# Token tile 0's scaling on ScalarE with its residual added by a transfer, and the last tile's VectorE steps in another order

## The chip, the cores and the metric

The kernel runs on one core of one Trainium2 chip. Its time is device microseconds of one execution, and the median of several runs is quoted. Below, PE is TensorE, ACT is ScalarE, DVE is VectorE, POOL is GpSimd and SP is SyncE, which here only starts transfers.

## What is computed

One layer of an encoder trunk on 512 tokens of width 1024, in float32: a mixer and a feed-forward block, each with a root-mean-square norm before and behind it and a residual around it. What matters here is the last statement:

```python
h2 = _rmsnorm(x, g_pre_ffn)
x = x + _rmsnorm(_conv_gated_mlp(h2, w_up, conv_w, conv_b, w_down), g_post_ffn)
```

with `_rmsnorm(z, g) = z * rsqrt(mean(z * z) + EPS) * g`. So each row of the down projection's product z is squared and summed over its 1024 columns, one power gives its scale, and the row times the weights g times the scale is added to the residual row of x (called x1 in the kernel) and stored.

## The kernel before

The 512 tokens are four tiles of 128 rows, called tokens 0 to 3 in the code and here, and the 1024 columns are two halves of 512. All products are float32 made of three products of split operands, and TensorE runs through nearly the whole program. The down projection comes last, first for columns 0 to 511, then for columns 512 to 1023, each half by a Strassen-like scheme of seven products whose sums lie in eight PSUM banks. The second half ends with `token(t)`, called in the order 0, 2, 1, 3: token 0 inside `after6`, between two of the scheme's last products, the others behind the last product. Each call first starts the loads of the residual rows x1 from DRAM (line 1440, on SP's queue), then issues 24 matmuls (`add_whole`, line 1370) that complete two banks, 12 matmuls for each, and then the norm:

- `sums(i)` for i = 0, 1: DVE adds a PSUM bank and a partial sum to z (line 1452, 256 columns), ACT squares it and sums along the row (line 1454).
- `weighted(i)`: DVE multiplies z by the norm's weights into zs (line 1459).
- `first_sum()` (line 1462) and `scale()` (lines 1469 and 1470): DVE adds the four partial sums of squares in two steps (tiles q and qs, one column wide), and POOL raises the result to the power -0.5 (tile qr).
- `rows(...)`: DVE multiplies by the scale and adds the residual (line 1502), for columns 0 to 511 (tile zg) and 512 to 1023 (tile zs); each result is then stored (line 1505), from SP's queue or ACT's.

`rows` of one token is called within the next token's call; `ahead` carries what it needs. Columns 0 to 511 (zg) were weighted earlier, while the second half's products ran. A framework puts semaphores between engines and may reorder, but `keep_in_program_order` (`pin`) holds DVE's steps of tokens 1 and 3 as they are written. Each engine works through its own instructions in program order, and a transfer's start is one of them on SP, ACT or POOL. The names on DVE: q_8045, q_8047, q_8046 and q_8048 belong to tokens 0, 2, 1, 3, and so do zg_8240, zg_8368, zg_8304 and zg_8432.

Of the kernel before, what the change touches and what calls it, by code (L numbers as in the profile page):

```python
# [12 lines left out]
AF = mybir.ActivationFunctionType  # L13
ALU = mybir.AluOpType
# [3 lines left out]
S = 512  # L18
# [31 lines left out]
def tile_block(ctx: ExitStack, tc, xT, x, wall, par, cs, wsp, bsp, gpost, gffn, out):  # L50
    nc = tc.nc
# [10 lines left out]
    def blk(dt=F32, n="blk", shape=(P, S)):  # L62
        return sb.tile(list(shape), dt, tag="blk", bufs=NBLK, name=nm(n))
# [17 lines left out]
    def tmp(n="tmp", shape=(P, S)):  # L81
        return sb.tile(list(shape), F32, tag="tmp", bufs=6, name=nm(n))

    def halves(n):
        return [blk(n=n), blk(n=n)]

    def small(n, w, bufs=2):
        return sb.tile([P, w], F32, tag=n, bufs=bufs, name=nm(n))
# [4 lines left out]
    def const(n, shape):  # L93
        return sb.tile(list(shape), F32, tag=n, bufs=1, name=n)
# [182 lines left out]
    def w_get(look=LOOK):  # L277

        i = w_pos[0]
        w_pos[0] += 1  # L280
        room = 2 * look + (2 if w_size(units[i]) == 2 else 0)
        n = sum(w_size(u) for u in units[i : w_pos[1]])
        while w_pos[1] < len(units) and (w_pos[1] <= i or n + w_size(units[w_pos[1]]) <= max(room, 9 if look == LOOK else 0)):
            u = units[w_pos[1]]
            w_ready[w_pos[1]] = w_unit(u)
            w_pos[1] += 1
            n += w_size(u)
        return w_ready.pop(i)
# [106 lines left out]
    for k in range(KD):  # L395
# [4 lines left out]
        xt = xts[k]  # L400
# [55 lines left out]
    for t in range(NT):  # L456
        for n in range(2):
            xt = blk(n="x0")
            nc.sync.dma_start(xt, x[t, :, n * S : (n + 1) * S])
            nc.scalar.activation(  # L460
                out=xt, in_=xt, func=AF.Square, accum_out=ss[:, 4 * n + t : 4 * n + t + 1]
# [18 lines left out]
    for c in range(19, 1, -2):  # L480
        v.scalar_tensor_tensor(
            out=lc, in0=lc, scalar=1.0 / c, in1=lb, op0=ALU.add, op1=ALU.mult
        )
    v.scalar_tensor_tensor(out=lc, in0=lc, scalar=1.0, in1=la, op0=ALU.add, op1=ALU.mult)
    with behind():
        v.tensor_scalar(out=lg, in0=lgt, scalar1=0.0, scalar2=None, op0=ALU.min)
    v.scalar_tensor_tensor(
        out=lg, in0=lc, scalar=-2.0, in1=lg, op0=ALU.mult, op1=ALU.add
# [12 lines left out]
    for i, op in enumerate((ALU.max, ALU.min)):  # L501
        v.tensor_scalar(
            out=near[:, i * P : (i + 1) * P], in0=dist[:, P : 2 * P], scalar1=0.0, scalar2=None, op0=op
# [5 lines left out]
    zt = const("zt", [P, H, NT])  # L509
# [605 lines left out]
    x1 = [[dp_.tile([P, S], F32, tag=f"x1_{t}{n}", name=f"x1_{t}{n}") for n in range(2)] for t in range(NT)]  # L1115
# [36 lines left out]
    def turn(t, zs):  # L1152
        c = slice(t * 64, (t + 1) * 64)
        pf = []
        for n in range(2):
            p = ps()
            for f in range(4):
                pf.append(p[:, f * P : (f + 1) * P])
                nc.tensor.transpose(pf[-1], zs[n][:, f * P : (f + 1) * P], ident)
        for k in range(KD):  # L1160
            high = nc.scalar.activation(
                out=two(h2h[k])[:, :, c], in_=in_turn(pf[k]), func=AF.Copy, scale=col(FFNG + k)
            )
        for k in range(KD):
            last = v.scalar_tensor_tensor(
                out=two(h2l[k])[:, :, c], in0=in_turn(pf[k]), scalar=col(FFNG + k), in1=as32(two(h2h[k])[:, :, c]),
                op0=ALU.mult, op1=ALU.subtract,
            )
        return pf, high.ins, last.ins
# [26 lines left out]
    for t in range(NT):  # L1196
        acc = [dn_.finish(t, 0)]
        if t > 1:
            rows, _, last = turn(t - 2, zs[t - 2])
            if t == 2:  # L1200
                h2_rows(0, rows)
            with tc.issue_after(last):
                zs[t - 1] = scaled(*zs[t - 1])
        acc.append(dn_.finish(t, 1))
        zs[t], squared, ended = norms(t, acc)
        if t == 0:
            zs[0] = scaled(*zs[0])
    with tc.issue_after(squared):
        h2_rows(1, rows)
# [150 lines left out]
    def add_whole(m, t, gs, ws, last=False):  # L1360

        c = slice(t * P, (t + 1) * P)
        for n, b in enumerate(((M2, M3), (M4, M8))[t // 2]):
            o = m[b][:, (t % 2) * 256 : (t % 2 + 1) * 256]
            for g, (wh, wl) in zip(gs, ws):
                for k in range(2):
                    f = slice(k * S + n * 256, k * S + (n + 1) * 256)
                    ah, al = whole[2 * g + k]
                    for i, (a_, w_) in enumerate(((ah, wh), (ah, wl), (al, wh))):
                        nc.tensor.matmul(  # L1370
                            o, a_[:, c], turns(w_[:, f]), start=b == M8 and t == 2 and g == k == i == 0,
                            stop=last and g == gs[-1] and k == 1 and i == 2, skip_group_check=True,
                        )
# [60 lines left out]
    def token(t):  # L1434

        if not ww:
            ww.extend([w_get(), w_get()])
        xt = halves("x1")
        for n in range(2):
            nc.sync.dma_start(xt[n], x1[t][n])  # L1440
        add_whole(m, t, (0, 1), ww, True)
        z, zs_ = blk(n="z"), blk(n="zs")
        last, ahead[:] = list(ahead), []
        banks = (((M2, e1), (M3, xx)), ((M4, uu), (M8, yy)))[t // 2]
        halves_ = slice(0, 256), slice(256, 512)
        end = t in (1, NT - 1)
        pin = tc.keep_in_program_order if end else (lambda i: i)

        def sums(i):
            b, e = banks[i]  # L1450
            f = halves_[t % 2]
            pin(v.tensor_add(z[:, halves_[i]], m[b][:, f], e[:, f]))
            j = tmp("junk")
            nc.scalar.activation(
                out=j[:, :256], in_=z[:, halves_[i]], func=AF.Square, scale=D ** -0.5, accum_out=qn[t][:, 2 + i : 3 + i]
            )

        def weighted(i):
            pin(v.tensor_mul(zs_[:, halves_[i]], z[:, halves_[i]], gpf[1][:, halves_[i]]))

        def first_sum():
            pin(v.scalar_tensor_tensor(
                out=qn[t][:, 0:1], in0=qn[t][:, 2:3], scalar=EPS, in1=qn[t][:, 0:1], op0=ALU.add, op1=ALU.add
            ))

        sc, s_2 = small("qr", 1, 4), small("qs", 1, 4)

        def scale():
            pin(v.tensor_add(s_2, qn[t][:, 0:1], qn[t][:, 3:4]))
            nc.gpsimd.tensor_tensor(out=sc, in0=s_2, in1=nhalf[:, 0:1], op=ALU.pow)  # L1470

        sums(0)
        if t == NT - 1:
            weighted(0)
            sums(1)
            first_sum()
            rows(*last, (0,), pin)
            scale()
            rows(*last, (1,), pin)
            weighted(1)  # L1480
        else:
            weighted(0)
            first_sum()
            if end:
                rows(*last, (0,), pin)
            sums(1)
            if last:
                rows(*last, (1,) if end else (0,), pin)
            scale()
            weighted(1)  # L1490
            if last and not end:
                rows(*last, (1,))
        ahead[:] = t, xt, zs_, sc

    def rows(t, xt, zs_, sc, which, pin=lambda i: i):

        zt = (zg[t], zs_)
        for i, (a, b) in enumerate(((0, 512), (512, 768), (768, 1024)) if t == NT - 1 else ((0, 512), (512, 1024))):
            if a // S in which:
                f = slice(a % S, a % S + b - a)  # L1500
                o = zt[a // S][:, f]
                pin(v.scalar_tensor_tensor(
                    out=o, in0=o, scalar=sc, in1=xt[a // S][:, f], op0=ALU.mult, op1=ALU.add
                ))
                (nc.sync, nc.scalar)[i % 2].dma_start(out[t, :, a:b], o)

    def after6():
        v.tensor_add(uu, m[M6], e1)
        v.tensor_sub(xx, m[M5], uu)
        token(0)  # L1510
# [15 lines left out]
    for t in (2, 1, 3):  # L1526
        token(t)
# [133 lines left out]
```

## Time and profile before

| What | Value |
|---|---|
| Median of 3 runs | 785.63 us |
| The runs | 784.94, 785.63, 787.22 us |
| The profiled execution | 785.08 us, its span 783.3 us |
| TensorE busy | 775.6 us, 99% of the span |
| VectorE busy | 626.5 us, 80% |
| ScalarE busy | 467.8 us, 60% |
| GpSimd busy | 104.0 us, 13% |
| Last matmul starts | 776.12 us after the span's start |

The span runs from the first to the last instruction, and 1.8 us of the execution lie around it. A timeline row has the start and the duration in us, the engine, the line, the operation, output and inputs, a shape, a count, and in brackets the engine's idle time before it with what ended it. Duration and start-to-start distance differ, since successive instructions of one engine overlap a little. "SPq" and "ACTq" rows are transfers being started. "Landing" is the time from a transfer's start to the completion of its data.

### The profile page before, as it was taken

The page shows a single profiled execution, that of the slowest core. Times are in us where ns is not written, and L with a number is a line of the kernel's source. Part 1 is how long each engine was busy: PE and PEld are TensorE (multiplying, and loading weights), DVE is VectorE, ACT ScalarE, POOL GpSimd, SP SyncE. Part 2 cuts the span into 40 slices and gives each one's busy share as a digit, 9 for nine tenths or more (in the row PEclk, how much of TensorE's full clock was granted, in tenths as well). Part 3 has the DMA queues.
Part 4 walks back from the last instruction along what each step waited for, and adds up shares of the span by engine and source line. Part 5 has one row for each costly group of instructions (what it writes and reads, how often), then busy time and mean ns, then how long its engine had stood idle before and what let it go on. Part 6 is the DMA issues. An engine that isn't in the chain of part 4 may idle for free.

```text
span 783.3 us, 13258 instructions
## 1 busy us (share of the span) xinstructions
PE 775.6 (99%) x5067; PEld 720.3 (92%) x5067; DVE 626.5 (80%) x1067; ACT 467.8 (60%) x848; POOL 104.0 (13%) x132
## 2 busy tenths in 40 slices
PE   9999999999999999999999999999999999999996
PEld 8888998998899999999998998999999998999996
DVE  7467887788786877867765679989999889877987
ACT  7555558689385544444444776657777578644542
POOL 0040001130012111032211200001111012200001
PEclk9999999999999999999999999999999999999999
DMA  8782224453123333223459111425555365632244
GB/s 293 260 266 88 81 82 162 108 133 126 55 106 108 108 108 108 106 84 108 138 161 344 57 69 39 122 108 141 141 149 149 108 196 114 170 114 108 108 162 162
DMA packets 35889, 104.78 MB, mean 134 GB/s; under 512 B 4401, under 2 KB 6321, under 8 KB 35825
## 3 DMA queue, kind: packets, MB, share of 16 engines
q1 hardware_dynamic: 27936, 87.81, 31.8%
q0 software_dynamic: 7024, 14.95, 9.0%
q10 hardware_dynamic: 864, 1.18, 0.4%
q8 instruction: 39, 0.64, 0.3%
q14 instruction: 26, 0.20, 0.1%
HBM read 91.34 MB, written 4.19 MB: 122 GB/s over the span
## 4 chain that ended last, share of the span: by engine, by line
PE 98%; DVE 1%; ACT 0%; POOLq 0%; issue 0%; POOL 0%; DVEq 0%
PE ps L917 22%; PE ps L291 13%; PE ps L293 13%; PE ps L292 13%; PE ps L1354 11%; PE ps L746 5%; PE ps L625 4%; PE ps L627 4%; PE ps L626 4%; PE ps L1089 2%; PE ps L1091 2%; PE ps L1090 2%; PE ps L1370 2%; PE ps L1011 1%; PE ps L411 1%; PE ps L393 0%
## 5 line engine op out<-in xcount | busy, mean ns | idle before, releaser
L116 DVE TENSOR_TENSOR wl<-raw,wh 128x1024 fp32r<-128x1024 f32 (+1 forms) x88 | 100.6, 1152 | 56.1 <-issue 20.6
L97 ACT ACTIVATE wf<-raw 128x512 fp32r<-128x512 f32 x126 | 75.6, 624 | 83.8 <-PE ps L292 37.1
L97 ACT ACTIVATE wh<-raw 128x1024 fp32r<-128x1024 f32 (+2 forms) x92 | 89.1, 981 | 28.9 <-DMA raw<-wall 15.5
L917 PE MATMUL ps<-sh,wf 128*128 128x256 f32 x576 | 105.3, 275 | 0.0
L116 DVE TENSOR_TENSOR wf<-raw,wf 128x512 fp32r<-128x512 f32 x126 | 93.3, 754 | 14.9 <-ACT wf L97 14.7
L917 PEld LDWEIGHTS ps<-sh,wf 128*128 128x128 f32 x576 | 91.7, 192 | 0.8 <-ACT u L97 0.2
L291 PE MATMUL ps<-h2h,wh 128*128 128x512 f32 (+1 forms) x256 | 90.7, 354 | 0.0
L293 PE MATMUL ps<-h2h,wl 128*128 128x512 f32 (+1 forms) x256 | 90.4, 353 | 0.0
L292 PE MATMUL ps<-h2l,wh 128*128 128x512 f32 (+1 forms) x256 | 90.4, 353 | 0.0
L917 PE MATMUL ps<-sl,wf 128*128 128x256 f32 x288 | 79.3, 275 | 0.0
L1354 PE MATMUL ps<-dh,fh 128*128 128x256 f32 x216 | 59.5, 276 | 0.0
L1354 PE MATMUL ps<-dh,fl 128*128 128x256 f32 x216 | 59.5, 275 | 0.0
L1354 PE MATMUL ps<-dl,fh 128*128 128x256 f32 x216 | 59.4, 275 | 0.0
L917 PEld LDWEIGHTS ps<-sl,wf 128*128 128x128 f32 x288 | 55.3, 192 | 0.4
L97 ACT ACTIVATE dh<-raw 128x768 fp32r<-128x768 f32 (+1 forms) x36 | 33.6, 950 | 33.5 <-DVE raw L224 17.6
L293 PEld LDWEIGHTS ps<-h2h,wl 128*128 128x128 f32 x256 | 48.6, 190 | 5.1
L291 PEld LDWEIGHTS ps<-h2h,wh 128*128 128x128 f32 x256 | 48.7, 190 | 4.5
L292 PEld LDWEIGHTS ps<-h2l,wh 128*128 128x128 f32 x256 | 48.7, 190 | 4.4
L627 PE MATMUL ps<-wh,xl 128*128 128x512 f32 x128 | 48.6, 379 | 0.0
L626 PE MATMUL ps<-wl,xh 128*128 128x512 f32 x128 | 48.5, 379 | 0.0
L625 PE MATMUL ps<-wh,xh 128*128 128x512 f32 x128 | 48.5, 380 | 0.0
L917 PE MATMUL ps<-xh,wf 128*128 128x256 f32 x240 | 43.8, 276 | 0.0
(343 smaller groups left out, 2185.8 us busy)
## 6 DMA issues: line engine op xcount, KB each, us to landing
raw<-wall SPq DMA_DIRECT2D x144, 512.0 KB, 3.6
x<-x SPq DMA_DIRECT2D x24, 256.0 KB, 5.9
fl<-gp POOLq DMA_DIRECT2D x12, 256.0 KB, 4.0
swap<-qkraw POOLq DMA_DIRECT2D x16, 128.0 KB, 4.3
x<-x POOLq DMA_DIRECT2D x8, 256.0 KB, 2.3
fl<-fs POOLq DMA_DIRECT2D x8, 256.0 KB, 3.3
xT<-xT SPq DMA_DIRECT2D x7, 256.0 KB, 5.5
xT<-xT POOLq DMA_DIRECT2D x4, 256.0 KB, 4.0
```

Source lines behind the costliest of these rows:

```text
L97: return nc.scalar.activation(out=o, in_=i, func=AF.Copy)
L116: low[0] = nc.vector.tensor_sub(lo, src, as32(hi)).ins
L291: nc.tensor.matmul(o, ah, bh, start=start, stop=False, skip_group_check=skip)
L292: nc.tensor.matmul(o, ah, bl, start=False, stop=False, skip_group_check=skip)
L293: nc.tensor.matmul(o, al, bh, start=False, stop=stop, skip_group_check=skip)
L625: nc.tensor.matmul(acc[t], xh[k][:, c], turns(wh[:, f]), start=k == 0, stop=False)
L626: nc.tensor.matmul(acc[t], xh[k][:, c], turns(wl[:, f]), start=False, stop=False)
L627: part_end[0] = nc.tensor.matmul(acc[t], xl[k][:, c], turns(wh[:, f]), start=False, stop=k == KD - 1)
L746: nc.tensor.matmul(bank[t], a_[:, c], turns(w_[:, f]), start=first and k == i == 0, stop=last and k == 3 and i == 2, skip_group_check=True,)
L917: self.last = nc.tensor.matmul(o, w_[:, c], a_, start=first and k == n == 0, stop=k == 3 and n == 2, skip_group_check=True,)
L1089: nc.tensor.matmul(o, ah, turns(bh), start=k == 0, stop=False)
L1354: nc.tensor.matmul(o, a_[:, c], turns(w_[:, f]), start=j == t == i == 0, stop=j == DP - 1 and i == 2 and n not in (M2, M3, M4), skip_group ...
```

## The change

Three things change. First, token 0's `rows` no longer use DVE: ACT multiplies zg and zs by the scale, in place (line 1501 of the changed kernel); POOL starts two transfers that add x1 from DRAM to them in SBUF (line 1502); and each is stored when its sum has landed (line 1503), zg from SP's queue, zs from ACT's. Second, the loads of token 0's residual rows into SBUF are gone. Third, in the last token (3), token 1's `rows` stand ahead of token 3's sums, one before each, and both `weighted` stand ahead of `scale`. Line numbers behind line 1501 are 7 higher in the changed kernel.

```diff
--- before.py
+++ after.py
@@ -1435,8 +1435,8 @@
 
         if not ww:
             ww.extend([w_get(), w_get()])
-        xt = halves("x1")
-        for n in range(2):
+        xt = halves("x1") if t else x1[t]
+        for n in range(2 if t else 0):
             nc.sync.dma_start(xt[n], x1[t][n])
         add_whole(m, t, (0, 1), ww, True)
         z, zs_ = blk(n="z"), blk(n="zs")
@@ -1469,16 +1469,17 @@
             pin(v.tensor_add(s_2, qn[t][:, 0:1], qn[t][:, 3:4]))
             nc.gpsimd.tensor_tensor(out=sc, in0=s_2, in1=nhalf[:, 0:1], op=ALU.pow)
 
-        sums(0)
         if t == NT - 1:
-            weighted(0)
+            rows(*last, (0,), pin)
+            sums(0)
+            rows(*last, (1,), pin)
             sums(1)
             first_sum()
-            rows(*last, (0,), pin)
+            weighted(0)
+            weighted(1)
             scale()
-            rows(*last, (1,), pin)
-            weighted(1)
         else:
+            sums(0)
             weighted(0)
             first_sum()
             if end:
@@ -1495,6 +1496,12 @@
     def rows(t, xt, zs_, sc, which, pin=lambda i: i):
 
         zt = (zg[t], zs_)
+        if t == 0:
+            for n in which:
+                nc.scalar.activation(out=zt[n], in_=zt[n], func=AF.Copy, scale=sc)
+                nc.gpsimd.dma_start(zt[n], xt[n], accum_op=ALU.add)
+                (nc.sync, nc.scalar)[n].dma_start(out[t, :, n * S : (n + 1) * S], zt[n])
+            return
         for i, (a, b) in enumerate(((0, 512), (512, 768), (768, 1024)) if t == NT - 1 else ((0, 512), (512, 1024))):
             if a // S in which:
                 f = slice(a % S, a % S + b - a)
```

On ACT, at the end of the program, before (junk is the square's unused output; line 1505 stores zs):

```order
L1454 ACTIVATE junk_8616,q_8045<-z_8611 128x256 [waits DVE_49]
L1454 ACTIVATE junk_8621,q_8045<-z_8611 128x256 [waits DVE_49]
L1454 ACTIVATE junk_8674,q_8047<-z_8669 128x256 [waits DVE_49]
L1505 DMA out<-zs_8612 128x512 [waits DVE_49]
L1454 ACTIVATE junk_8679,q_8047<-z_8669 128x256 [waits DVE_49]
L1454 ACTIVATE junk_8721,q_8046<-z_8716 128x256 [waits DVE_49]
L1454 ACTIVATE junk_8728,q_8046<-z_8716 128x256 [waits DVE_49]
L1505 DMA out<-zs_8670 128x512 [waits DMAHW2_49,DVE_49]
L1454 ACTIVATE junk_8768,q_8048<-z_8763 128x256 [waits DVE_49,Activation_49]
L1454 ACTIVATE junk_8772,q_8048<-z_8763 128x256 [waits DVE_49,Activation_49]
```

and after:

```order
L1501 ACTIVATE zg_8240<-zg_8240,qr_8609 128x512 [waits Pool_49]
L1501 ACTIVATE zs_8608<-zs_8608,qr_8609 128x512 [waits DVE_49]
L1454 ACTIVATE junk_8670,q_8047<-z_8665 128x256 [waits DVE_49]
L1454 ACTIVATE junk_8675,q_8047<-z_8665 128x256 [waits DVE_49]
L1503 DMA out<-zs_8608 128x512 [waits DMASW4_49]
L1454 ACTIVATE junk_8719,q_8046<-z_8714 128x256 [waits DVE_49]
L1454 ACTIVATE junk_8726,q_8046<-z_8714 128x256 [waits DVE_49]
L1512 DMA out<-zs_8666 128x512 [waits DMAHW0_49,DVE_49]
L1454 ACTIVATE junk_8768,q_8048<-z_8761 128x256 [waits DVE_49,Activation_49]
L1512 DMA out<-zs_8715 128x512 [waits DMAHW2_49,DVE_49]
L1454 ACTIVATE junk_8773,q_8048<-z_8761 128x256 [waits DVE_49,Activation_49]
```

Two scalings stand behind token 0's squares, and the store of token 0's zs now stands behind both of token 2's squares and ahead of token 1's, and waits for a transfer of POOL's (DMASW4) where it waited for DVE. The store of token 1's zs moved between token 3's two squares.

On DVE, from token 1's `scale` to the end, before:

```order
L1469 TENSOR_TENSOR qs_8719<-q_8046 128x1 [waits Activation_49]
L1459 TENSOR_TENSOR zs_8717<-z_8716,gpf_8117 128x256 [waits DVE_49]
L1452 TENSOR_TENSOR z_8763<-ps_8109,e_8050 128x256 [waits PE_49]
L1459 TENSOR_TENSOR zs_8764<-z_8763,gpf_8117 128x256 [waits DMASW5_49,DVE_49]
L1452 TENSOR_TENSOR z_8763<-ps_8640,e_8052 128x256 [waits PE_49]
L1462 SCALAR_TENSOR_TENSOR q_8048<-q_8048 128x1 [waits Activation_49]
L1502 SCALAR_TENSOR_TENSOR zg_8304<-zg_8304,qr_8718,x_1453_8688 128x512 [waits DMAHW4_49,Pool_49]
L1469 TENSOR_TENSOR qs_8766<-q_8048 128x1 [waits DVE_49,Activation_49]
L1502 SCALAR_TENSOR_TENSOR zs_8717<-zs_8717,qr_8718,x_1454_8689 128x512 [waits DMAHW6_49]
L1459 TENSOR_TENSOR zs_8764<-z_8763,gpf_8117 128x256
L1502 SCALAR_TENSOR_TENSOR zg_8432<-zg_8432,qr_8765,x_1461_8735 128x512 [waits DMAHW7_49,Pool_49]
```

and after:

```order
L1469 TENSOR_TENSOR qs_8717<-q_8046 128x1 [waits Activation_49]
L1459 TENSOR_TENSOR zs_8715<-z_8714,gpf_8117 128x256 [waits DVE_49]
L1509 SCALAR_TENSOR_TENSOR zg_8304<-zg_8304,qr_8716,x_1451_8686 128x512 [waits DMAHW1_49,Pool_49]
L1452 TENSOR_TENSOR z_8761<-ps_8109,e_8050 128x256 [waits PE_49]
L1509 SCALAR_TENSOR_TENSOR zs_8715<-zs_8715,qr_8716,x_1452_8687 128x512 [waits DMAHW2_49,DVE_49]
L1452 TENSOR_TENSOR z_8761<-ps_8636,e_8052 128x256 [waits PE_49]
L1462 SCALAR_TENSOR_TENSOR q_8048<-q_8048 128x1 [waits Activation_49]
L1459 TENSOR_TENSOR zs_8762<-z_8761,gpf_8117 128x256 [waits DVE_49] x2
L1469 TENSOR_TENSOR qs_8764<-q_8048 128x1 [waits DVE_49,Activation_49]
L1509 SCALAR_TENSOR_TENSOR zg_8432<-zg_8432,qr_8763,x_1459_8733 128x512 [waits DMAHW5_49,Pool_49]
```

Token 1's `rows` (zg_8304, zs_8715) are now ahead of token 3's two additions from PSUM (z_8761 from ps_8109 and ps_8636), and token 3's two weightings stand ahead of its last sum (qs_8764). Further up, token 0's two line-1502 steps are gone.

On SP, the end's residual loads and the store between them, before:

```order
L1440 DMA x_1436_8583<-x_00_4352 128x512 [waits DMASW5_49,PE_49]
L1440 DMA x_1437_8584<-x_01_4353 128x512 [waits DMASW6_49,DMASW0_49,PE_49]
L1440 DMA x_1445_8641<-x_20_4356 128x512 [waits DMASW1_49,PE_49]
L1440 DMA x_1446_8642<-x_21_4357 128x512 [waits DMASW2_49,DMASW0_49,PE_49]
L1505 DMA out<-zg_8240 128x512 [waits DVE_49]
L1440 DMA x_1453_8688<-x_10_4354 128x512 [waits DMASW5_49,DMASW7_49,DMASW2_49,DMAHW4_49,DMASW1_49,PE_49]
L1440 DMA x_1454_8689<-x_11_4355 128x512 [waits DMASW6_49,DMASW5_49,DMAHW6_49,DMASW3_49,PE_49]
L1440 DMA x_1461_8735<-x_30_4358 128x512 [waits DMAHW7_49,DMASW3_49,PE_49]
L1440 DMA x_1462_8736<-x_31_4359 128x512 [waits DMAHW0_49,DMASW4_49,PE_49]
```

and after:

```order
L1440 DMA x_1443_8637<-x_20_4356 128x512 [waits DMASW7_49,DMASW1_49,PE_49]
L1440 DMA x_1444_8638<-x_21_4357 128x512 [waits DMASW2_49,DMASW6_49,DMASW1_49,PE_49]
L1440 DMA x_1451_8686<-x_10_4354 128x512 [waits PE_49]
L1440 DMA x_1452_8687<-x_11_4355 128x512 [waits DMASW7_49,DMASW0_49,PE_49]
L1503 DMA out<-zg_8240 128x512 [waits DMASW3_49]
L1440 DMA x_1459_8733<-x_30_4358 128x512 [waits DMASW6_49,DMAHW5_49,DMASW4_49,PE_49]
L1440 DMA x_1460_8734<-x_31_4359 128x512 [waits DMASW2_49,DMAHW6_49,DMASW0_49,PE_49]
```

Token 1's loads (x_10, x_11) moved ahead of the store of token 0's zg, and token 3's (x_30, x_31) still stand behind it; that store now waits for POOL's first transfer (DMASW3).

On POOL, token 0's two transfers stand between its power and token 2's.

## The prediction

> **What bounds the kernel now.** I read the page first, then the chain that ended last, then the timelines of the last 20 us engine by engine. From the page, the span and the chain's shares by engine:
>
> ```profile
> span 783.3 us, 13258 instructions
> PE 98%; DVE 1%; ACT 0%; POOLq 0%; issue 0%; POOL 0%; DVEq 0%
> ```
>
> TensorE carries 98% of the chain, and the change leaves its instructions alone. So only what follows TensorE can move, and how late that is shows in two rows of its timeline (the matmul that completes token 1's first bank, and the program's last, which completes token 3's second bank):
>
> ```profile
> 772.10 0.28 PE L1370 MATMUL ps<-wh,fl 128*128 128x256 f32 x1
> ...
> 776.12 0.28 PE L1370 MATMUL ps<-wh,fl 128*128 128x256 f32 x1
> ```
>
> The banks are complete at 772.38 and 776.40. The span ends 6.9 us after that. DVE's timeline there (the first row is one of token 0's two residual steps):
>
> ```profile
> 769.35 0.75 DVE L1502 SCALAR_TENSOR_TENSOR zg<-zg,qr,x 128x512 f32<-128x512 f32 x1
> ...
> 773.48 0.16 DVE L1462 SCALAR_TENSOR_TENSOR q<-q 128x1 f32<-128x1 f32 x1
> 773.57 0.75 DVE L1502 SCALAR_TENSOR_TENSOR zg<-zg,qr,x 128x512 f32<-128x512 f32 x1
> ...
> 775.24 0.16 DVE L1469 TENSOR_TENSOR qs<-q 128x1 f32<-128x1 f32 x1
> 775.31 0.42 DVE L1459 TENSOR_TENSOR zs<-z,gpf 128x256 f32<-128x256 f32 x1
> 775.64 0.42 DVE L1452 TENSOR_TENSOR z<-ps,e 128x256 f32<-128x256 f32 x1
> ...
> 776.44 0.42 DVE L1452 TENSOR_TENSOR z<-ps,e 128x256 f32<-128x256 f32 x1
> ...
> 777.51 0.16 DVE L1469 TENSOR_TENSOR qs<-q 128x1 f32<-128x1 f32 x1
> 777.58 0.74 DVE L1502 SCALAR_TENSOR_TENSOR zs<-zs,qr,x 128x512 f32<-128x512 f32 x1
> 778.25 0.42 DVE L1459 TENSOR_TENSOR zs<-z,gpf 128x256 f32<-128x256 f32 x1
> 778.77 0.75 DVE L1502 SCALAR_TENSOR_TENSOR zg<-zg,qr,x 128x512 f32<-128x512 f32 x1
> ```
>
> Three things are to be seen. Token 3's last addition runs at 776.44, 0.04 us after its matmul ends: before the change DVE keeps pace with TensorE. Successive steps start 0.33 us (256 columns, 775.31 to 775.64) or 0.67 us (512, 777.58 to 778.25) apart. And while token 1's power is taken (behind 775.24) DVE adds token 3's first bank at 775.64, so that wait costs nothing. From 776.44 on everything is one chain: addition, square, sum, power, token 3's `rows`, stores. In it stand ACT's square and POOL's power (the chain of waits, in order of time):
>
> ```profile
> 772.94 0.52 ACT junk L1454 x2
> ...
> 776.95 0.53 ACT junk L1454 x2
> ...
> 777.78 0.96 POOLq L1657
> ```
>
> The last row covers the power, 0.93 us there, where others are shorter (POOL's timeline):
>
> ```profile
> 768.76 0.56 POOL L1470 TENSOR_TENSOR qr<-qs,nhalf 128x1 f32<-128x1 f32 x1 [84.89 <-DVE qs L1469]
> 772.72 0.55 POOL L1470 TENSOR_TENSOR qr<-qs,nhalf 128x1 f32<-128x1 f32 x1 [3.40 <-DVE qs L1469]
> 775.54 0.60 POOL L1470 TENSOR_TENSOR qr<-qs,nhalf 128x1 f32<-128x1 f32 x1 [2.27 <-DVE qs L1469]
> 777.81 0.93 POOL L1470 TENSOR_TENSOR qr<-qs,nhalf 128x1 f32<-128x1 f32 x1 [1.67 <-DVE qs L1469]
> ```
>
> **Part 1: token 0 leaves DVE.** Two steps, 2 x 0.67 = 1.34 us of DVE, go. That buys next to nothing: token 2's and token 1's sums then wait for TensorE. Token 1's first addition can start at 772.42 at the earliest (772.38 + 0.04); its square starts 0.45 us later if ACT is free, 772.87 against 772.94 now. Gain at most 0.07 us; I count none. The two loads that go were complete before 769.35, where the step that used them ran, and held nobody up: nothing.
>
> **Part 2: ACT's scalings and POOL's transfers.** The power of token 0 ends at 768.76 + 0.56 = 769.32, so ACT scales zg from 769.35. The nearest rows are other scalings of 128x512 on ACT followed by accumulating transfers on POOL (line 1255, also 256 KB):
>
> ```profile
> 670.58 0.64 ACT L1254 ACTIVATE fl<-fh 128x512 fp32r<-128x512 f32 x1
> ...
> 671.57 0.85 POOL L1255 DMA_DIRECT2D fl<-fs  x1 [4.40 <-DVE cv L1232]
> ...
> 672.74 0.87 POOL L1255 DMA_DIRECT2D fl<-gp  x1 [0.32 <-ACT fl L1254]
> ```
>
> POOL starts 0.99 us after the scaling starts (671.57 - 670.58): zg's transfer at 770.34. Its issue takes 0.87 us, so zs's starts at 771.21, since zs is scaled by then. The scalings hold ACT until about 770.5, where token 2's first square starts now (ACT's timeline, and below it the time that starting a store takes there):
>
> ```profile
> 770.47 0.42 ACT L1454 ACTIVATE junk<-z 128x256 f32<-128x256 f32 x1 [2.45 <-DVE z L1452]
> ...
> 771.13 0.38 ACTq L1505 DMA_DIRECT2D out<-zs  x1
> ```
>
> POOL is free again at 772.1, ahead of token 2's power (772.72). No cost on either. How long the transfers take (issues of that stage; the first and the second of the pair):
>
> ```profile
> fl<-fs POOLq DMA_DIRECT2D x1, 256.0 KB, 3.3
> fl<-gp POOLq DMA_DIRECT2D x1, 256.0 KB, 4.6
> ```
>
> The first lands at 671.57 + 3.3 = 674.9, the second at 677.3; it comes out behind the first. All accumulating transfers of line 1255 landed in:
>
> ```profile
> DMA to landing us min/median/max: 2.8/3.5/5.7
> ```
>
> Here the two follow each other at 0.87 us. For zs I take 4.4 us, near the second of that pair: landing at 775.6. The ends are 3.3 (a lone one) and 5.7 (the longest).
>
> **Part 3: the wait this adds on ACT.** ACT's store of zs waits for that landing, and token 1's two squares are queued behind it on ACT. Whether a transfer's start holds what stands behind it shows on SP, where four loads, which themselves wait only for long finished matmuls of line 1354 and earlier transfers, stood behind the store of zg:
>
> ```profile
> 770.13 0.34 SPq L1505 DMA_DIRECT2D out<-zg  x1
> 770.69 1.85 SPq L1440 DMA_DIRECT2D x<-x  x4
> ```
>
> They went only after it. How soon ACT goes on after a landing shows in a row where it waited for an accumulating transfer (issued at 662.84, landing 3.3 later):
>
> ```profile
> 662.84 0.86 POOL L1255 DMA_DIRECT2D fl<-fs  x1 [6.05 <-DVE gp L1274]
> ...
> 666.18 0.42 ACT L97 ACTIVATE fa<-gp 128x256 fp32r<-128x256 f32 x1 [0.22 <-DMA fl<-fs]
> ```
>
> That is 0.04 us. Then ACT starts the store, 0.38 us. So token 1's first square starts at 775.6 + 0.04 + 0.38 = 776.02 instead of 772.94: **3.08 us later**. DVE's in-order `first_sum` of token 1 (773.48 now) waits for it, and all of DVE's tail is queued behind that step. By 776.02 TensorE is all but done and covers nothing more. At the ends of the landing the shift is 1.98 (3.3) and 4.38 us (5.7).
>
> **Part 4: token 3's order on DVE.** Times below are on the old clock, without that shift. Token 1's sum stays at 775.24 and its power ends at 775.54 + 0.60 = 776.14. Now token 1's `rows` for zg is DVE's next step: it waits until 776.17, and token 3's first addition, which filled this gap, comes behind it at 776.84. Then token 1's zs at 777.18, token 3's second addition at 777.85 (776.44 now), `first_sum` at 778.19, the weightings at 778.28 and 778.61. The second square needs that addition's end (778.27) and ACT, which first starts the store of token 1's zs (its step ends at 777.92, plus 0.38: 778.30); 0.56 us later, as 776.95 to 777.51 now, its sum is there at 778.86. DVE comes to `scale` at 778.95, against 777.51: +1.44. The power starts 0.30 us later as now, but DVE is idle, so I take 0.56 instead of 0.93 us: zg of token 3 starts at 778.95 + 0.30 + 0.56 + 0.03 = 779.84 against 778.77, **1.07 us later**. The ends are 1.07 and, with 0.93, 1.44.
>
> The long power runs beside DVE steps with two SBUF inputs (777.58, 778.25). The Trainium skill, "SBUF — State Buffer", "SBUF: two separate sides", says that such a DVE instruction and a GpSimd one that reads SBUF lock each other out of a shared port for a whole instruction. By that rule the power is short again here and the sum stays; without it 0.37 us would be added.
>
> **Part 5: what else waits.** SP's store of zg waits for the first landing, 770.34 + 3.3 = 773.6. Token 3's loads stand behind it and start at 774.0 and 774.5. At the longest landing of such a load (line 1440 gives 2.7 to 5.7 us),
>
> ```profile
> DMA to landing us min/median/max: 2.7/4.9/5.7
> ```
>
> they land by 780.2; DVE wants them at 779.84 + 3.08 = 782.9. Hidden, with 2.7 us to spare. Behind token 3's `rows` all is as before: two steps, then stores.
>
> **The sum.** 3.08 + 1.07 = 4.15 us. The profiled execution took 785.08 us (its span and 1.78 us around it) and would take 789.2; it lies 0.55 us below the median of the runs, from which the same sum gives 789.8. I say 789.5. What this measurement can tell from no change is about 0.3%, 2.36 us.
>
> **The rivals.**
> 1. *The transfer lands quickly.* Against it: the lone accumulating transfer above took 3.3 us. For it: DMA is idle just before token 0's transfers start (the last columns of the stage's row in the table of windows: granted clock 1.00, DMA share 0.00, 0 GB/s), and POOL's plain 256 KB transfers of line 1137 take
>
> ```profile
> 764.00:770.00 6.00, 6.00 (x57) 6.00 (x56) 5.13 (x11) 1.02 (x4) 0.56 (x1) 1.00 0.00 0
> ```
>
> ```profile
> L1137 POOL DMA_DIRECT2D x<-x x8: 539/558/589, 427.8 to 453.8; - x8
> ...
> DMA to landing us min/median/max: 2.3/2.3/2.8
> ```
>
> With 0.3 us more issue (0.85 instead of 0.56), 2.6 us: landing 773.81, shift 1.29, sum 2.36, time 787.4. With 3.3 us the sum is 3.05, 788.1 to 788.7. Chance 17%. The Trainium skill, "DMA: Bandwidth & Descriptors", "Anatomy of one DMA", gives 2.0 us plus bytes at 436 GB/s for a transfer of this path, an estimate of 2.6 us for 256 KB; by it the time is this rival's 787.4, but the rows above show 3.3 and 4.6.
> 2. *Not slower: ACT's squares pass the waiting store.* If ACT's store does not hold the squares behind it, or the transfer lands before they are wanted (by 772.94 - 0.42 = 772.5, 1.3 us after its start), only part 4 is left: +1.07, 786.2 to 786.7, within 0.3%. SP's rows speak against the first, every landing above against the second. 10%.
> 3. *Faster: DVE's tail shortens.* The freed 1.34 us would have to reach the chain behind 776.44. That chain needs one addition, square, sum, power and token 3's `rows`; only the power's 0.37 us can go, so 784.7 at best, and no gain of 0.3%. 2% for what I don't see.
> 4. *The transfers or token 3's loads come later still* (5.7 us or more, as where a DMA queue is busy): 5.45 us or more, 790.5 and up. 6%.
>
> **How the numbers follow.** The forecast has 65%. Its own range is 788.1 (a landing of 3.3) to 791.1 (785.63 + 5.45). The whole range takes in rival 1's low end, 787.4, and leaves out rivals 2 and 3 and part of 4: 787.4 to 791.1. Slower by over 0.3%: the forecast, rival 4 and most of rival 1, 86%. Within 0.3%: rival 2 and the rest of rival 1, 12%. Faster: 2%.
>
> **What would show it.** Right: ACT's first square of token 1 starts directly after the store of zs, near 776, with idle time before it that ends with POOL's transfer; DVE's `first_sum` of token 1 at about 776.6; a gap on DVE ahead of token 1's zg, of about 0.5 us, and token 3's second addition 4.5 us after TensorE's end; the last power near 0.56 us. Wrong: squares of token 1 near 772.9 (rival 2), or landings of under 3 us (rival 1).

## The result, and the profile after

The changed kernel takes 790.83 us, the median of 6 runs (790.21 to 792.77). The kernel before took 785.86 us beside it (median of 6, 784.94 to 787.22). The two medians differ by 5.0 us. The ratio of the runs is given as 1.0071, with a 95% interval of 1.006 to 1.0082; it is a little above the quotient of these medians (1.0063), and stands for 5.6 us (4.7 to 6.4). So the change makes the kernel slower, and the runs below show that it does so by the mechanism that was forecast. The size is off: 789.5 us had been said, and 785.63 us, from which the prediction counted, times the ratio is 791.2 us, just above the top of its whole range (791.1).

The profiled execution took 790.5 us. Its page, the span and the chain's shares by engine:

```profile
span 788.7 us, 13257 instructions
PE 97%; DVE 1%; DMA 1%; issue 0%; POOL 0%; DVEq 0%; POOLq 0%; ACT 0%; ACTq 0%
```

A transfer now stands in the chain, and the chain in order of time shows which one and what follows it:

```profile
771.41 5.33 DMA zs<-x
776.74 0.02 issue
776.76 0.35 ACTq L1503
777.11 0.05 issue
777.16 0.52 ACT junk L1454 x2
```

Token 0's second transfer (zs) takes 5.33 us, then ACT starts its store, then come token 1's two squares. This is part 3 of the prediction. ACT's timeline has the wait itself, and DVE's the step that waits for the square:

```profile
769.71 0.72 ACT L1501 ACTIVATE zg<-zg,qr 128x512 f32<-128x512 f32 x1 [1.33 <-POOL qr L1470]
...
776.76 0.35 ACTq L1503 DMA_DIRECT2D out<-zs  x1
777.16 0.42 ACT L1454 ACTIVATE junk<-z 128x256 f32<-128x256 f32 x1 [4.64 <-DMA zs<-x]
```

```profile
777.70 0.16 DVE L1462 SCALAR_TENSOR_TENSOR q<-q 128x1 f32<-128x1 f32 x1 [4.05 <-ACT junk L1454]
...
780.39 0.75 DVE L1509 SCALAR_TENSOR_TENSOR zg<-zg,qr,x 128x512 f32<-128x512 f32 x1 [0.44 <-POOL qr L1470]
781.06 0.42 DVE L1452 TENSOR_TENSOR z<-ps,e 128x256 f32<-128x256 f32 x1
...
782.05 0.42 DVE L1452 TENSOR_TENSOR z<-ps,e 128x256 f32<-128x256 f32 x1
...
783.15 0.16 DVE L1469 TENSOR_TENSOR qs<-q 128x1 f32<-128x1 f32 x1
784.04 0.75 DVE L1509 SCALAR_TENSOR_TENSOR zg<-zg,qr,x 128x512 f32<-128x512 f32 x1 [0.73 <-POOL qr L1470]
784.71 0.88 DVE L1509 SCALAR_TENSOR_TENSOR zs<-zs,qr,x 128x256 f32<-128x256 f32 x2
```

DVE stands idle for 4.05 us, and later for 0.44 us ahead of token 1's zg (780.39), because token 3's first addition (781.06) now comes behind that step. POOL's timeline and the landings in this stretch (line, count, size of one, median us to landing):

```profile
770.79 0.92 POOL L1502 DMA_DIRECT2D zg<-x  x1 [1.12 <-ACT zg L1501]
771.41 1.22 POOL L1502 DMA_DIRECT2D zs<-x  x1
772.86 0.56 POOL L1470 TENSOR_TENSOR qr<-qs,nhalf 128x1 f32<-128x1 f32 x1 [0.23 <-DVE qs L1469]
...
783.46 0.55 POOL L1470 TENSOR_TENSOR qr<-qs,nhalf 128x1 f32<-128x1 f32 x1 [3.10 <-DVE qs L1469]
```

```profile
x<-x SPq DMA_DIRECT2D x2, 256.0 KB, 3.6
zg<-x POOLq DMA_DIRECT2D x1, 256.0 KB, 4.3
zs<-x POOLq DMA_DIRECT2D x1, 256.0 KB, 5.3
```

To compare traces, times are taken against TensorE's end (the last matmul's start plus 0.28 us), because that end lies anywhere from 776.04 to 778.53 us in the runs below. Here it is 776.76:

```profile
776.48 0.28 PE L1370 MATMUL ps<-wh,fl 128*128 128x256 f32 x1
```

DVE's last row before the change was:

```profile
779.44 0.87 DVE L1502 SCALAR_TENSOR_TENSOR zs<-zs,qr,x 128x256 f32<-128x256 f32 x2
```

Before, token 1's first square started 3.46 us ahead of TensorE's end (772.94 against 776.40), and DVE ended 3.91 us behind it (779.44 + 0.87 = 780.31). Now the square starts 0.40 us behind that end, which is 3.86 us later. DVE ends 8.83 us behind it (785.59), which is 4.92 us later. The other 1.06 us is put down to token 3's order here, and runs below take the two apart. TensorE's end is 0.36 us later in this execution and the end behind DVE 0.12 us longer, so the span's 5.4 us are accounted for.

### The profile page after: what moved, and what is told of

Same layout as the page of the kernel before. It is cut to its first block, busy times and chain, and to the rows that moved or that the text cites. A ratio compares the mean times of both kernels' runs of the same rounds, so it can differ in the third digit from the quotient of the medians.

```text
span 788.7 us, 13257 instructions
## 1 busy us (share of the span) xinstructions
PE 775.8 (98%) x5067; PEld 719.4 (91%) x5067; DVE 625.7 (79%) x1065; ACT 468.7 (59%) x850; POOL 105.7 (13%) x134
## 4 chain that ended last, share of the span: by engine, by line
PE 97%; DVE 1%; DMA 1%; issue 0%; POOL 0%; DVEq 0%; POOLq 0%; ACT 0%; ACTq 0%
PE ps L917 21%; PE ps L291 13%; PE ps L293 13%; PE ps L292 13%; PE ps L1354 11%; PE ps L746 5%; PE ps L625 4%; PE ps L627 4%; PE ps L626 4%; PE ps L1089 2%; PE ps L1090 2%; PE ps L1091 2%; PE ps L1370 2%; PE ps L1011 1%; PE ps L411 1%; DMA zs<-x 1%
```

## The experiments

The theory: all of the loss is what stands in program order behind a start that waits (3.9 us), plus token 3's order (1.1 us). The rivals: the transfers or the traffic cost in themselves, and the landing is long for another reason than its source and its place as the second of a pair. Every ratio is to the kernel before on the same chip; rows and landings are of one execution of each run.

**The store of zs held back.** The changed kernel, with ACT's store of token 0's zs behind token 3's second square:

```diff
-                (nc.sync, nc.scalar)[n].dma_start(out[t, :, n * S : (n + 1) * S], zt[n])
+                store = lambda n=n: (nc.sync, nc.scalar)[n].dma_start(out[t, :, n * S : (n + 1) * S], zt[n])
+                held.append(store) if n else store()
...
             scale()
+            with tc.issue_after(square[0]):
+                held.pop()()
```

> The changed kernel, but ACT's store of token 0's zs is held until behind token 3's second square. Theory (token 1's squares wait behind that store for POOL's second transfer, and token 3's order costs 1.05 us beside it): token 1's first square starts within 0.4 us of 772.9 again, the landings stay near 4.3 and 5.3 us, and only the order is left: about 1.05 us over the kernel before, some 786.9 us. Rival (the transfers cost by themselves, or by token 3's loads, which stand behind the other store on SP): the time stays over 789 us.

Measured: 787.52 us (median of 10), ratio 1.0027 [1.0017, 1.0036]. ACT's timeline of this run:

```profile
772.91 0.42 ACT L1454 ACTIVATE junk<-z 128x256 f32<-128x256 f32 x1 [0.71 <-DVE z L1452]
...
778.49 0.60 ACTq L1505 DMA_DIRECT2D out<-zs  x1
```

The transfers land as slowly as before (4.2 and 5.1 us), and yet the square is back where it was, 3.53 us ahead of TensorE's end (776.44). DVE ends 1.00 us late instead of 4.92. So the 3.9 us are not the transfer. They are the order of the work behind its waiting store. The store that was put off is not free either: from the start of the last store to the span's end this run takes 3.52 us, against 2.96 before. The order's 1.00 us and these 0.56 make the 1.6 us by which the profiled execution's span is longer than before; it is the fastest of the ten. The median is 2.2 us over the kernel before, where 1.05 had been expected.

**Token 3's order alone**, in the kernel before:

```diff
-        sums(0)
         if t == NT - 1:
-            weighted(0)
-            sums(1)
-            first_sum()
             rows(*last, (0,), pin)
-            scale()
+            sums(0)
             rows(*last, (1,), pin)
+            sums(1)
+            first_sum()
+            weighted(0)
             weighted(1)
+            scale()
         else:
+            sums(0)
```

> The kernel before with token 3's new order on DVE alone. Theory: token 1's step for zg waits for its power with nothing in front of it, token 3's second addition starts about 1.4 us later than in the kernel before, the last power takes 0.55 instead of 0.93 us: 1.05 us slower, about 786.9 us. Rival (the order only pays, by the shorter power): 0.4 us faster, about 785.5 us.

Measured: 786.67 us (median of 11), ratio 1.0019 [1.001, 1.0027]. POOL's last power, ACT's second square of token 3, and what DVE does behind it:

```profile
780.70 0.55 POOL L1470 TENSOR_TENSOR qr<-qs,nhalf 128x1 f32<-128x1 f32 x1 [3.39 <-DVE qs L1469]
```

```profile
779.86 0.42 ACT L1454 ACTIVATE junk<-z 128x256 f32<-128x256 f32 x1 [0.82 <-DVE zs L1459]
```

```profile
779.01 0.42 DVE L1452 TENSOR_TENSOR z<-ps,e 128x256 f32<-128x256 f32 x1
...
780.40 0.16 DVE L1469 TENSOR_TENSOR qs<-q 128x1 f32<-128x1 f32 x1 [0.23 <-ACT junk L1454]
```

DVE ends 1.35 us later against TensorE's end. The order costs about what was worked out, and 0.3 us more here: the square starts 0.43 us after z is complete (779.43), where it starts 0.14 us after it in the changed kernel (782.61 against 782.05 + 0.42). Its row names DVE's weighting of z (line 1459), whose output the square does not read. Two other runs below have the same 0.3 us with another step named, so what the square waits for stays open. The power is short, as forecast.

**Token 3's order undone** in the changed kernel (its steps as in the kernel before, the rest of the change kept):

```diff
         if t == NT - 1:
-            rows(*last, (0,), pin)
             sums(0)
-            rows(*last, (1,), pin)
+            weighted(0)
             sums(1)
             first_sum()
-            weighted(0)
-            weighted(1)
+            rows(*last, (0,), pin)
             scale()
+            rows(*last, (1,), pin)
+            weighted(1)
```

> The changed kernel with token 3's old order. Theory: the wait behind the store remains, the order's share goes: 1.05 us faster than the changed kernel, about 789.8 us, 3.9 to 4.3 us over the kernel before. Rival (the order matters only where the store's wait is absent, since everything is late anyway): no faster than the changed kernel, 790.8 us.

Measured: 789.19 us (median of 5), ratio 1.0049 [1.0037, 1.0062]. Landings of 4.1 and 5.6 us. The square starts 0.68 us behind TensorE's end, 4.14 later than before, and DVE ends 4.12 us later: the wait alone, with nothing added. POOL's last power is long again:

```profile
782.33 0.93 POOL L1470 TENSOR_TENSOR qr<-qs,nhalf 128x1 f32<-128x1 f32 x1 [1.66 <-DVE qs L1469]
```

**Both undone**: the store held back as in the first run, and the old order as in the third (the diffs above together).

> The changed kernel with the store of zs held until behind token 3's second square, and with token 3's old order: ACT's scalings and POOL's transfers remain. Theory: as the kernel before, 785.9 us, up to 0.6 us more if token 3's loads, which still stand behind the store of zg on SP, come late. Rival (the transfers or the scalings cost by themselves): over 788 us.

Measured: 787.26 us (median of 7), ratio 1.0028 [1.0017, 1.0039]. That is no better than the first run, though the new order is gone. Its profiled execution is the slowest of the seven (789.22 us), so it shows what can go wrong and not the typical size. DVE's and SP's timelines:

```profile
781.72 0.75 DVE L1512 SCALAR_TENSOR_TENSOR zg<-zg,qr,x 128x512 f32<-128x512 f32 x1 [0.65 <-DMA x<-x]
```

```profile
776.88 0.34 SPq L1505 DMA_DIRECT2D out<-zg  x1
777.38 0.82 SPq L1440 DMA_DIRECT2D x<-x  x2
```

Token 3's residual loads wait on SP behind the store of zg, which waits for the first transfer. With the rest of the tail early, DVE now waits for them (0.65 us of idle). In the changed kernel this wait is hidden because the tail is late anyway.

**The residual from SBUF.** The changed kernel, with token 0's residual rows loaded into SBUF as before, so that the two transfers add from SBUF:

```diff
-        xt = halves("x1") if t else x1[t]
-        for n in range(2 if t else 0):
+        xt = halves("x1")
+        for n in range(2):
```

> The changed kernel, but token 0's residual rows are loaded into SBUF as before the change, and POOL's two transfers add from there instead of from DRAM. Theory 1 (a source in DRAM makes these transfers a microsecond longer than the ones of line 1255, whose source is in SBUF): landings of about 3.3 and 4.4 us, about 1 us faster than the changed kernel, 789.8 us. Theory 2 (two transfers started at nearly the same time delay each other): landings stay at 4.3 and 5.3 us, 790.8 us.

Measured: 789.22 us (median of 4), ratio 1.0052 [1.0037, 1.0067]. The landings and ACT's wait:

```profile
zg<-x POOLq DMA_DIRECT2D x1, 256.0 KB, 3.4
zs<-x POOLq DMA_DIRECT2D x1, 256.0 KB, 4.2
```

```profile
775.44 0.42 ACT L1454 ACTIVATE junk<-z 128x256 f32<-128x256 f32 x1 [3.62 <-DMA zs<-x]
```

These are, within 0.2 us, the 3.3 and 4.4 us that the prediction took by the rows of line 1255. The rows quoted there had an SBUF source, and the change has a DRAM source: that is the 0.9 us by which the landing was mis-sized. The square starts 1.03 us earlier against TensorE's end (0.63 ahead of 776.07) than in the changed kernel, and DVE ends 1.04 us earlier.

**One transfer instead of two**: zg stays on DVE, with its rows loaded; only zs goes by ACT and POOL.

```diff
-        xt = halves("x1") if t else x1[t]
-        for n in range(2 if t else 0):
+        xt = halves("x1") if t else [blk(n="x1"), x1[t][1]]
+        for n in range(2 if t else 1):
...
-        if t == 0:
+        if t == 0 and which == (1,):
```

> The changed kernel, but zg of token 0 is scaled and added by DVE as before the change; only zs goes by ACT and POOL. Theory 1 (source in DRAM): the lone transfer lands after 4.3 us, starts about 0.6 us earlier, and the time is about 1.6 us under the changed kernel, 789.2 us. Theory 2 (two delay each other): it lands after 3.3 us, about 2.6 us under the changed kernel, 788.2 us.

Measured: 789.80 us (median of 4), ratio 1.006 [1.0045, 1.0075]. The lone transfer, started at 770.07, lands in 5.5 us, which fits neither expectation. SP's timeline shows what was not foreseen, four loads of 256 KB beside the transfer:

```profile
770.20 1.91 SPq L1440 DMA_DIRECT2D x<-x  x4
```

So this run settles nothing by itself, and the last run repeats it without those loads.

**Transfers that don't add.** The same two transfers without `accum_op`, so the sum is left out:

```diff
-                nc.gpsimd.dma_start(zt[n], xt[n], accum_op=ALU.add)
+                nc.gpsimd.dma_start(zt[n], xt[n])
```

> The changed kernel with POOL's two transfers overwriting zg and zs instead of adding to them, so that token 0's rows come out as the residual alone: the sum is left out. If the addition inside the transfer makes it long, the landings fall to about 2.3 and 3 us and the time by about 2.3 us, to 788.5 us. If the source or the pair does, they stay above 4 and 5 us and the time at 790.8 us.

Measured: 788.60 us (median of 4), ratio 1.0042 [1.0027, 1.0057]. The starts on POOL and the landings:

```profile
771.62 0.58 POOL L1502 DMA_DIRECT2D zg<-x  x1 [1.11 <-ACT zg L1501]
772.20 0.55 POOL L1502 DMA_DIRECT2D zs<-x  x1
```

```profile
zg<-x POOLq DMA_DIRECT2D x1, 256.0 KB, 3.0
zs<-x POOLq DMA_DIRECT2D x1, 256.0 KB, 3.1
```

Adding costs 1.3 us on the first landing and 2.2 us on the second. Without it the second follows the first without loss. The square comes 2.32 us earlier against TensorE's end than in the changed kernel, and DVE ends 2.34 us earlier.

**zs first.** zs is scaled and transferred ahead of zg:

```diff
-            for n in which:
+            for n in (1 - n for n in which):
```

> The changed kernel with token 0's zs scaled and transferred before zg. Theory (ACT is held until zs has landed, and not by the pair): zs lands first, about 1.6 us earlier than in the changed kernel, and the time falls by the same 1.6 us, to about 789.2 us. Rival (both transfers must be over, or the loads on SP behind zg's store decide): no change, 790.8 us.

Measured: 788.69 us (median of 4), ratio 1.0045 [1.0028, 1.0061]. The landings have changed places:

```profile
zs<-x POOLq DMA_DIRECT2D x1, 256.0 KB, 4.3
zg<-x POOLq DMA_DIRECT2D x1, 256.0 KB, 5.4
```

So it is the second of the pair that is 1 us longer, whichever tile it fills, and ACT waits for zs alone. The square starts 1.27 us ahead of TensorE's end, 1.67 earlier than in the changed kernel, and DVE ends 1.69 us earlier.

**Everything moved out from behind the transfers.** Token 0 stays on ACT and the transfers; the residual loads of tokens 2, 1 and 3 stand at token 0; both stores of token 0 are SP's, the one of zs behind token 2's store of zg; token 3 in its old order:

```diff
+        if t == 0:
+            for u in (2, 1, 3):
+                xts_[u] = halves("x1")
+                for n in range(2):
+                    nc.sync.dma_start(xts_[u][n], x1[u][n])
+        xt = xts_[t]
...
+            with tc.issue_after(stored[2, 0]):
+                held.pop()()
...
-                (nc.sync, nc.scalar)[n].dma_start(out[t, :, n * S : (n + 1) * S], zt[n])
+                store = lambda n=n: nc.sync.dma_start(out[t, :, n * S : (n + 1) * S], zt[n])
+                held.append(store) if n else store()
```

> Edit to the changed kernel: token 0 stays on ScalarE and the transfers, but nothing is left behind them. The residual loads of tokens 2, 1 and 3 are all issued at token 0, ahead of zg's store on SP; zs's store goes from ACT's queue to SP's, behind token 2's store of zg; token 3's steps stand in their old order. Theory (all of the loss is what stands in order behind a waiting start, plus the new order): token 1's first square at TensorE's end less 3.4 to 3.5 us as before, token 3's steps on DVE as before, last power 0.93 us, about 3 us from DVE's end to the span's end; time within 1 us of the kernel before, ratio 0.999 to 1.0015. Rival (the transfers cost in themselves, through DMA traffic or more stores late on one queue): the landings are as long as in the other runs, the end behind DVE is 0.5 us or more longer, ratio 1.002 to 1.003.

Measured: 786.73 us (median of 11), ratio 1.0019 [1.0011, 1.0028]. Most of the loss is gone, but not all, and the interval leaves room for both numbers that were expected; the trace says what is left. The square is 3.47 us ahead of TensorE's end (776.08), as before the change. DVE ends 0.87 us later against that end. POOL's timeline shows one cause:

```profile
772.01 1.21 POOL L1507 DMA_DIRECT2D zs<-x  x1
772.79 1.02 POOL L1473 TENSOR_TENSOR qr<-qs,nhalf 128x1 f32<-128x1 f32 x1
```

Token 2's power ends at 773.81. It ends 0.59 us after the second transfer's start is through (772.01 + 1.21 = 773.22), which is the length of a power, so it most likely waited for that start, though the row counts the wait as its own time. DVE's step for token 2's zg (773.84) waited for it, 0.53 us, and is 0.59 us later against TensorE's end than before. The changed kernel has no such collision. It comes up here because DVE does token 0's sums (line 1455) behind an addition of the Strassen-like scheme that waits for TensorE, where the changed kernel does them ahead of it:

```profile
767.40 0.69 DVE L1526 TENSOR_TENSOR e<-ps,e 128x512 f32<-128x512 f32 x1 [1.86 <-PE ps L1354]
768.01 0.75 DVE L1455 TENSOR_TENSOR z<-ps,e 128x256 f32<-128x256 f32 x2
```

So both transfers start 1.28 us later against TensorE's end (zs's 4.07 us ahead of it, 5.35 in the changed kernel). The edit does not ask for this reordering, and its share says little of the transfers as such. The other 0.29 us of the 0.87 is the open wait of the run with the order alone: token 3's second square starts 0.38 us after z is complete (0.39 with both undone), against 0.09 before. Then the end: from the last store's start (780.89) to the span's end this run takes 3.51 us, against 2.96 before and 3.08 in the changed kernel. The two other runs that put a 256 KB store off to the end show the same or more (3.52 and, with both undone, 4.12); those that don't stay at 2.91 to 3.14. So in these runs the stores that token 0's transfers delay go with about half a microsecond more at the end. That is the part in which the rival was right. No variant here beats the kernel before.

**One transfer with no load beside it**: as the run with one transfer, with all residual loads at token 0:

```diff
+        if t == 0:
+            xts_[0] = [blk(n="x1"), x1[0][1]]
+            nc.sync.dma_start(xts_[0][0], x1[0][0])
+            for u in (2, 1, 3):
+                xts_[u] = halves("x1")
+                for n in range(2):
+                    nc.sync.dma_start(xts_[u][n], x1[u][n])
...
-        if t == 0:
+        if t == 0 and which == (1,):
```

> Edit to the changed kernel: only zs goes by ScalarE and a transfer, zg stays on VectorE, as in the run with one transfer, but all residual loads are issued at token 0's start, so that no load runs beside the lone transfer; token 3's steps stay in the new order, and zs's store stands on ACT behind token 1's first square. Theory (an accumulating transfer from DRAM takes 4.3 us alone, and 1 us more as the second of a pair): the lone transfer lands in 4.1 to 4.4 us; the 5.5 us of the run with one transfer came from the four loads beside it. Rival (zs's 5.3 us is a matter of its place or its buffer, not of being second): 5 us or more. Rival (the pair slows both): 3.5 us or less. Time: with the square ahead of the store only token 1's second square waits, ratio 1.001 to 1.005; it decides nothing.

Measured: 788.45 us (median of 4), ratio 1.0045 [1.003, 1.006]. The landing:

```profile
zs<-x POOLq DMA_DIRECT2D x1, 256.0 KB, 4.3
```

So a lone adding transfer of 256 KB from DRAM takes 4.3 us here, 5.5 where four loads were beside it, and 5.3 with another adding transfer 0.6 us ahead of it. A store beside it does not show: SP starts one of 256 KB at 772.49, within this landing, and it is 4.3 us all the same.

The runs that differ in when zs lands lie on one line, and the last row, where the store stands elsewhere, leaves it (times against TensorE's end):

| Run | Landing of zs | Token 1's first square | DVE's end |
|---|---|---|---|
| Changed kernel | 5.3 us | +0.40 | +8.83 |
| From SBUF | 4.2 us | -0.63 | +7.79 |
| zs first (starts 0.62 us sooner) | 4.3 us | -1.27 | +7.14 |
| Not adding | 3.1 us | -1.92 | +6.49 |
| Store held back | 5.1 us | -3.53 | +4.91 |

Each microsecond by which zs lands later is a microsecond of DVE's end, as long as the squares stand behind the store.

## Why the prediction was right or wrong

- **Part 1 (DVE's freed steps buy nothing)** held. Where ACT is not held up, token 1's first square starts 3.53 and 3.47 us ahead of TensorE's end, against 3.46 before: 0.07 us at most.
- **Part 2 (scalings and transfers)** held up to the landing. ACT scales zg at 769.71, 0.36 us later than said, as TensorE is here. POOL starts the first transfer 1.08 us later (0.99 was taken) and the second 0.62 us after that (0.87 was taken). POOL is free at 772.63, ahead of token 2's power at 772.86. That it costs nothing on POOL is true of this kernel by 0.23 us; with the transfers 1.28 us later, as in the run with everything moved, it is not.
- **The term that failed is the landing in part 2**: 4.4 us for the second transfer and 3.3 for the first, against 5.3 and 4.3. The rows of line 1255 were read as the same kind, since they add 256 KB on POOL, but their source is in SBUF. The run from SBUF gives the 3.4 and 4.2, the one without adding 3.0 and 3.1, and the lone transfer from DRAM with no load beside it 4.3. The value of 4.4 was also below the 4.6 of the row that it was taken from. The bound of 5.7 covered the landing, the value taken did not. Nor were these the nearest rows: the kernel before has adding transfers of 256 KB from DRAM at line 264, which the prediction leaves out without a reason. The first of its four, started at 162.15, and then all four:

```profile
sb<-wall POOLq DMA_DIRECT2D x1, 256.0 KB, 3.8
```

```profile
DMA to landing us min/median/max: 3.8/6.0/9.8
```

The second, started 2.2 us behind the first, took 4.0 us; the third and fourth, started close behind it, took 8.0 and 9.8, with two loads of 512 KB beside them from 166.66 on. They point to a longer landing than 4.4 us for a second one close behind the first, but do not give the 5.3.

- **What the sum moves by.** With the landing as it was, and the small differences of the two starts, the sum goes from 4.15 to 4.92 us. The profiled executions differ by 5.42 us. The other 0.5 us, TensorE's end 0.36 us later and 0.12 us more behind DVE, the sum had at nothing; TensorE's end differs by more than this between the runs above (776.04 to 778.53), so it is not laid to the change.
- **Part 3 (the store holds the squares)** is the mechanism, and it was right, shown by the row of 4.64 us and by the run with the store held back. Its size was 3.08 us and is 3.86. The 0.78 us between them is, but for 0.01, the landing's 0.93 less the 0.25 that the second transfer started sooner after the first, plus the 0.09 by which the first started later.
- **Part 4 (token 3's order)**: 1.07 us was said, and 1.06 is what is left of DVE's 4.92 us. Undone alone it gives back 0.80 us of DVE's end (4.92 to 4.12, with a square that is 0.28 us later there), and alone it costs 1.35. The gap on DVE ahead of token 1's zg is 0.44 us, where about 0.5 was said. The last power is 0.55 us where DVE stands idle beside it, and 0.92 or 0.93 in the three runs with the old order, beside DVE's steps with two SBUF inputs. By the rule of the Trainium skill, "SBUF — State Buffer", "SBUF: two separate sides", that was to be expected, and the last power agrees with it in every trace here.
- **Part 5 (what else waits)** held in the changed kernel: token 3's loads start at 775.60, land 3.6 us later at the median, and are wanted at 784.04. What the prediction did not say is that the cover is made of the delay itself. With the delay and the new order both gone, DVE waited for these loads in the execution that was profiled.
- **The rivals.** The quick landing is refuted: not even the transfer without adding lands in 2.6 us here. The Trainium skill, "DMA: Bandwidth & Descriptors", "Anatomy of one DMA", gives 2.6 us by the prediction's estimate; a plain transfer from DRAM took 3.0 here, one that adds 4.3 and the kernel's own second one 5.3, so the skill's figure is too low for a transfer that adds. That the squares pass the waiting store is refuted by the 4.64 us. The same section of the Trainium skill says that a wait for a semaphore takes place on the sequencer that issues the transfer, and that is what ACT shows. The rival of later landings was given 5.45 us or more; the changed kernel came to 5.0 on the medians, between it and the forecast, and to 5.6 by the ratio, which reaches it. Its landing of 5.7 us or more was not there (5.3).

## What to carry to other kernels

A transfer's start that must wait holds everything behind it on its engine, so its place in the program counts as much as its length: behind a slow transfer, put its store on a queue and at a place where no computation and no load stands behind it. To size a transfer, take a row of the same kind in all respects, its source too: here one that adds took 3.4 us from SBUF and 4.3 from DRAM, and rows with a DRAM source stood elsewhere in the same program. And a step that is "hidden" should be asked what hides it; if that is the very delay that one means to remove, it comes back as the next bound.

## What was not expected of the hardware

- An adding transfer of 256 KB on POOL's queue takes 4.1 to 4.3 us from DRAM at the program's end (3.8 for the first of line 264) and 3.4 from SBUF, and one that doesn't add 3.0 (DRAM). A second adding one started 0.6 us behind the first takes about 1 us longer or more (5.1 to 5.9 in six executions, and 4.2 from SBUF); a second plain one does not (3.1).
- Its start holds POOL for 0.92 us, the second's 1.22 us, and a plain one for 0.55 to 0.58 us.
- Four loads of 256 KB beside a lone adding transfer go with 5.5 us where 4.3 was taken without them.
- ACT's multiplication of 128x512 by a scale per row takes 0.72 us, where the scalings at line 1254 took 0.64.
